# Head projections by pairs of output blocks, half of each sum by seven products of 256 tokens

## The chip, the cores and the metric

The kernel runs on one core of a Trainium2 chip. The metric is the device time of one execution in microseconds (us). A core has five engines that run side by side: PE multiplies matrices (128 x 128 weights against up to 512 columns, sums in PSUM), DVE and ACT work element by element on SBUF and PSUM, POOL does so on SBUF and issues transfers, SP issues transfers.

## The reference, cut to what matters

A decoder block on 512 tokens of width 2048, all in float32:

```python
hn = rmsnorm(h, norm1_g[l])
proj = hn @ w_in[l]                       # 2048 x 5656
(q_a, k_a, v_a, q_b, k_c, v_c, k_s, v_s, k_w, v_w, g_b) = jnp.split(proj, offsets, axis=-1)
o_a = dilated_mixture(...)                # 8 heads of 128
o_b = gates[..., 0:1] * o_cmp + gates[..., 1:2] * o_sel + gates[..., 2:3] * o_win   # 8 heads, 2 K/V groups
mixed = jnp.concatenate([rmsnorm(o_a, grp_norm_a[l]), rmsnorm(o_b, grp_norm_b[l])], axis=-1)
h = h + mixed @ w_out[l]
hn2 = rmsnorm(h, norm2_g[l])
h = h + (jax.nn.silu(hn2 @ w_gate[l]) * (hn2 @ w_up[l])) @ w_down[l]
return rmsnorm(h, final_g)
```

The compressed keys and values of mixer B come from `k_c` and `v_c` through a small two-layer network (weights `cmp_w1`, `cmp_w2`).

## The kernel before

**Precision.** Every operand of a large matrix product is kept as a high part and a rest (`wh`, `wl` for weights, `ah`, `al` for tokens), and a product is three matmuls: wh with ah, wh with al, wl with ah (`mm3`, `mm`). ACT makes the high part of a weight block (L143), DVE the rest (L146).

**The stream of weights.** All weights arrive in the order that `plan()` writes: units of 512 KB in one of five `raw` buffers, issued by SP (`load_to`). A unit is two halves; each half is a `Job` whose `first` (ACT) is written three halves ahead of its use and whose `second` (DVE) two halves ahead (`split_to`, called by `next_half`). `later(n, f)` puts other work n halves on. Every engine works through its own instructions strictly in the order written.

**The stages.** (1) The tokens are split into `ah`, `al` (16 slices of 128 features, 512 tokens each) while the projections for compression run. (2) The keys and values of the first group of mixer B (`ks`, `kw`, `vs`, `vw`), with sixteen units of compression weights (`w1_unit`) between their blocks. (3) The heads: for j from 0 to 7 four output blocks `qb`, `qa`, `ka`, `va`; at j = 4 also the second group's `ks`, `kw`, `vs`, `vw`. (4) The output projection, half of mixer B first (`out_unit(1)`) and that of mixer A afterwards. (5) The FFN, whose products are already formed by seven products of 256 tokens instead of eight (Strassen's scheme in Winograd's form: weight blocks and token blocks are added first, the quarter results afterwards). (6) The final norm.

**Stage 3 closely.** A block is one PSUM bank (`proj_block`, two of them) that takes 16 slices x 3 matmuls of 512 columns (`in_unit`, `run_unit`). After every six matmuls `side_hook` runs one `step()` of the attention: scores (`Att.s`), softmax rows on DVE and ACT, transposes (`Att.t`), the product with the values (`pv`). `evac` and `evac_v` take a finished block out of PSUM. When a head is done, `head_done` copies its output to `osb`, an SBUF tile that holds all sixteen, and sums its squares on POOL (L707). In the last block the outputs of mixer B are scaled and split into `ah`, `al` (`split_act`, L290 and L291), where the output projection reads them; after the last attention step (`close_attention`) those of mixer A follow.

Of the kernel before, what the change touches and what calls it, by code (L numbers as in the profile page):

```python
# [11 lines left out]
F32 = mybir.dt.float32  # L12
F32R = mybir.dt.float32r
AF = mybir.ActivationFunctionType
# [27 lines left out]

def plan():
# [9 lines left out]
    for j in range(NH):  # L53
        if j == 4:
            for name in ("ks", "kw", "vs", "vw"):
                for half in range(2):
                    p.append(("in", name, 1, half))
        for name in ("qb", "qa", "ka", "va"):
            for half in range(2):
                p.append(("in", name, j, half))  # L60
# [12 lines left out]

@with_exitstack
def block_kernel(ctx: ExitStack, tc: tile.TileContext, xt, wst, wdn, smalls, wg, w2c, bias, ident_in, out):
# [8 lines left out]
    mem = ctx.enter_context(tc.tile_pool(name="mem", bufs=1, space=bass.MemoryType.DRAM))  # L84
    kept_hs = [mem.tile([128, S], F32, name=f"res{nb}") for nb in range(KB)]
# [44 lines left out]
    class Job:  # L130
# [3 lines left out]
        def __init__(self, src, prep=None, post=None, load=None, dst=None, even=False):  # L134
            self.src, self.prep, self.post, self.load, self.dst, self.even = src, prep, post, load, dst, even

        def first(self):
            if self.load:
                self.load()
            if self.prep:  # L140
                self.prep()
            self.h, self.l = self.dst() if self.dst else wsplit(self.even)
            act.activation(self.h, self.src(), AF.Copy)  # L143

        def second(self):
            dve.tensor_tensor(self.l, self.src(), self.h.bitcast(F32), op=OP.subtract)  # L146
            if self.post:
                self.post()
# [27 lines left out]

    for u, d in enumerate(units):
        if d[0] not in ("quad", "dn"):
# [3 lines left out]
    n_plain = len(jobs)  # L182
    k = 2 * units.index(("out", 0, 1))
# [16 lines left out]

    pos = {"half": 0}
    side_hook = [lambda: None]

    def next_half():
# [3 lines left out]
        if i < n_plain:  # L208
            load_to(i // 2 + LA)
# [78 lines left out]
    def split_act(i, src, gain):  # L288
# [7 lines left out]
    osb = ap_.tile([128, KB, S], F32, name="osb")  # L296
# [9 lines left out]
    w2 = osb[:, 0, :].rearrange("p (a b) -> p a b", a=4)  # L306
    hids = osb[:, 1, :].rearrange("p (s h) -> p s h", s=2)
    hidt = [osb[:, 2, :128].rearrange("p (a r b) -> p a r b", a=2, r=1),
            osb[:, 3, :384].rearrange("p (a g r b) -> p a g r b", a=2, g=2, r=3)]
# [80 lines left out]

    def task():
        (tasks.popleft() if tasks else kv_low)()
# [79 lines left out]

    def evac(p, tag, scale=None, keep=False):
# [13 lines left out]
    def evac_v(p):  # L487
        t = tmp()
        dve.tensor_tensor(t, p, r1, op=OP.mult)
        return t  # L490
# [18 lines left out]
    class Att:  # L509


        def __init__(self, kind, q, k, v, bias_t, gate, o, first, last, done=None):
            self.kind, self.q, self.k, self.v, self.bias = kind, q, k, v, bias_t
            self.gate, self.o, self.first, self.last, self.done = gate, o, first, last, done
            self.e = {}
            self.s_steps = [self.cmp_s] if kind == "cmp" else [lambda: self.s([3]), lambda: self.s([2]),
                                                               lambda: self.s([1, 0])]
            self.t_steps = [self.cmp_t, self.cmp_pv] if kind == "cmp" else [
                lambda: self.t([3]), lambda: self.t([2]), lambda: self.t([1, 0]), self.pv]

# [9 lines left out]
        def s(self, tiles):  # L530
# [30 lines left out]
            later(0, rows)  # L561

        def t(self, tiles):
            p = ps.tile([128, 512], F32, tag="t", name="pt", bufs=2)
# [30 lines left out]
        def cmp_s(self):  # L595
# [23 lines left out]
            later(0, rows)  # L619

        def cmp_t(self):
            p = ps.tile([128, 512], F32, tag="t", name="pt", bufs=2)
# [6 lines left out]
        def cmp_pv(self):  # L629

            self.o["p"] = ps.tile([128, 512], F32, tag="o", name="po")
            pe.matmul(self.o["p"], self.v(), et_h[:96, 0:4, :], start=True, stop=False)

# [63 lines left out]
    def head_done(i, grp):  # L697
        def f(p):
            act.activation(osb[:, i, :], p, AF.Copy)
# [12 lines left out]

    kv = {}
    n1 = 0

    def kv_group(g, w1):
        nonlocal n1
        for name in ("ks", "kw", "vs", "vw"):
            p = proj_block()
            for half in range(2):  # L720
                in_unit(p, half)
# [11 lines left out]
            if name[0] == "k":  # L733
                kv[name] = evac(p, name)
            else:
                kv[name] = V()
                t = evac_v(p)
                queue.append(lambda t=t, name=name, v=kv[name]: setattr(v, "x", v_turn(t, name)))
# [13 lines left out]
    for j in range(NH):  # L752
# [5 lines left out]
        p = proj_block()  # L758
        for half in range(2):
            in_unit(p, half)  # L760
        q = evac(p, "qb", SCALE, True)
        o = {}
        queue.append(Att("cmp", q, kc[:, 32 * g:32 * g + 32],
                         V(et_h[:96, 7 + 3 * g, :]), bb, 3 * j, o, True, False))
        queue.append(Att("sel", q, kv["ks"], kv["vs"], bb, 3 * j + 1, o, False, False))
        queue.append(Att("win", q, kv["kw"], kv["vw"], bb, 3 * j + 2, o, False, True, head_done(8 + j, 1)))
        p = proj_block()
        for half in range(2):
            in_unit(p, half)
        q = evac(p, "qa", SCALE)  # L770
        p = proj_block()
        for half in range(2):
            in_unit(p, half)
        k = evac(p, "ka")
        v = V()
        queue.append(Att("dil", q, k, v, ba, None, {}, True, True, head_done(j, 0)))
        p = proj_block()
        for half in range(2):
            in_unit(p, half)
            if j == NH - 1 and half == 0:  # L780
                cur["late"] = 1
                for i in range(8):
# [760 lines left out]
```

## Time and profile before

| | |
|---|---|
| median of 3 runs | 2131.9 us (2131.46 to 2132.48) |
| profiled execution | 2134.17 us, its span 2132.1 us |
| granted PE clock | 0.998 |
| busy: PE, DVE, ACT, POOL | 2119.3, 1654.0, 1259.9, 316.9 us |
| moved from and to memory | 245.43 MB read, 65.01 MB written |

The span reaches from the first to the last instruction. A busy share is an average over stages; what an engine costs is read within one stage. The start times of two matmuls that follow each other without a wait give PE's real pace; their durations overlap. In the heads the tile names are `pp` (projection blocks), `psc` (scores), `pt` (transposed probabilities), `po` (head outputs), `pv` (transposed values); `pab` is the output projection, `phid` the compression, `P` and `pd` the FFN.

### The profile page before, as it was taken

To read this page: it belongs to the slowest core of one execution; us is meant where nothing else is said; L and a number is where in the kernel's file an instruction comes from. 1 tells how busy PE (TensorE), PEld (TensorE's weight loads), DVE (VectorE), ACT (ScalarE), POOL (GpSimd) and SP (SyncE) were. 2 spreads that over 40 slices of the span, in tenths; PEclk is the share of its full clock that TensorE was granted. 3 is DMA by queue.
4 is the path that set the end of the run, shared out by engine and by line. 5 is a ranking of instruction groups with operands and counts; after the bars stand their busy time and mean duration, and the time that the engine had idled before them with its cause. 6 is when DMAs were issued, how large, how long until landed. Compare 5 with 4: busy or idle time off the path is not lost.

```text
span 2132.1 us, 41370 instructions
## 1 busy us (share of the span) xinstructions
PE 2119.3 (99%) x15298; PEld 1980.7 (93%) x15298; DVE 1654.0 (78%) x3540; ACT 1259.9 (59%) x3059; POOL 316.9 (15%) x375
## 2 busy tenths in 40 slices
PE   9999999999999999999999999999999999999997
PEld 8888888888888888999999999999999999999997
DVE  6755656366557678998989888988888898988885
ACT  6544444244445246576676758585757667675856
POOL 0000000000000002011131413130312212030323
PEclk9999999999999999999999999999999999999999
DMA  7442222321224336356695959694756757494982
GB/s 238 145 144 82 82 82 70 101 82 51 87 95 148 99 99 171 119 164 197 150 208 152 231 138 221 154 206 131 186 145 169 180 139 185 138 218 118 210 245 92
DMA packets 122907, 313.13 MB, mean 147 GB/s; under 512 B 13264, under 2 KB 35408, under 8 KB 122704
## 3 DMA queue, kind: packets, MB, share of 16 engines
q1 hardware_dynamic: 75952, 236.49, 34.8%
q0 software_dynamic: 46608, 73.95, 19.5%
q8 instruction: 119, 1.95, 0.4%
q14 instruction: 84, 0.69, 0.1%
q10 hardware_dynamic: 144, 0.07, 0.0%
HBM read 245.43 MB, written 65.01 MB: 146 GB/s over the span
## 4 chain that ended last, share of the span: by engine, by line
PE 99%; DVE 0%; issue 0%; ACT 0%; DVEq 0%
PE P L1224 18%; PE P L1223 18%; PE P L1222 18%; PE pp L197 7%; PE pp L199 7%; PE pp L198 7%; PE pab L198 3%; PE pab L199 3%; PE pab L197 3%; PE pd L1222 1%; PE pd L1224 1%; PE pd L1223 1%; PE pt L568 1%; PE pl L198 1%; PE po L198 1%; PE po L197 1%
## 5 line engine op out<-in xcount | busy, mean ns | idle before, releaser
L143 ACT ACTIVATE wh<-raw 128x512 fp32r<-128x512 f32 x888 | 533.0, 625 | 279.1 <-DVE raw L810 118.9
L146 DVE TENSOR_TENSOR wl<-raw,wh 128x512 fp32r<-128x512 f32 x888 | 598.7, 685 | 101.5 <-ACT wh L143 98.5
L1224 PE MATMUL P<-ah,wl 128*128 128x256 f32 x1616 | 448.1, 277 | 0.0
L1222 PE MATMUL P<-ah,wh 128*128 128x256 f32 x1616 | 447.6, 277 | 0.0
L1223 PE MATMUL P<-al,wh 128*128 128x256 f32 x1616 | 447.3, 277 | 0.0
L1224 PEld LDWEIGHTS P<-ah,wl 128*128 128x128 f32 x1616 | 303.5, 188 | 0.7 <-DVE wl L146 0.2
L1222 PEld LDWEIGHTS P<-ah,wh 128*128 128x128 f32 x1616 | 303.5, 188 | 0.0
L1223 PEld LDWEIGHTS P<-al,wh 128*128 128x128 f32 x1616 | 303.5, 188 | 0.0
L1144 POOL DMA_DIRECT2D sums<-stg x240 | 201.0, 889 | 429.1 <-ACT P L1137 150.9
L197 PE MATMUL pp<-ah,wh 128*128 128x512 f32 x640 | 260.5, 407 | 0.0
L199 PE MATMUL pp<-ah,wl 128*128 128x512 f32 x640 | 250.9, 392 | 0.0
L198 PE MATMUL pp<-al,wh 128*128 128x512 f32 x640 | 250.2, 391 | 0.0
L170 DVE TENSOR_TENSOR wl<-raw,wh 128x256 fp32r<-128x256 f32 x480 | 186.5, 419 | 30.0 <-ACT wh L166 28.1
L810 DVE TENSOR_TENSOR raw<-raw 128x512 f32<-128x512 f32 x274 | 188.1, 686 | 3.6
L166 ACT ACTIVATE wh<-raw 128x256 fp32r<-128x256 f32 x480 | 176.6, 409 | 4.8 <-DVE raw L886 4.8
L199 PEld LDWEIGHTS pp<-ah,wl 128*128 128x128 f32 x640 | 120.2, 188 | 28.3 <-DVE wl L146 0.4
L197 PEld LDWEIGHTS pp<-ah,wh 128*128 128x128 f32 x640 | 120.5, 188 | 20.0 <-DVE tmp L369 0.5
L198 PEld LDWEIGHTS pp<-al,wh 128*128 128x128 f32 x640 | 120.6, 188 | 19.5
L555 ACT ACTIVATE e<-e,st 128x512 f32<-128x512 f32 (+1 forms) x96 | 53.7, 560 | 124.2 <-DVE st L549 124.2
L1137 ACT ACTIVATE stg<-P 128x256 f32<-128x256 f32 x280 | 106.7, 382 | 14.2 <-PE P L1224 2.7
L707 POOL TENSOR_TENSOR acc<-acc,osq 128x512 f32<-128x512 f32 x14 | 18.1, 1290 | 580.3 <-ACT osq L706 580.3
L197 PE MATMUL pab<-ah,wh 128*128 128x512 f32 x256 | 100.3, 392 | 0.0
(343 smaller groups left out, 5394.2 us busy)
## 6 DMA issues: line engine op xcount, KB each, us to landing
raw<-in_wst_dram SPq DMA_DIRECT2D x390, 512.0 KB, 4.2
sums<-stg POOLq DMA_DIRECT2D x160, 256.0 KB, 6.6
raw<-in_wst_dram POOLq DMA_DIRECT2D x40, 256.0 KB, 4.6
sums<-stg POOLq DMA_DIRECT2D x80, 128.0 KB, 6.2
bias<-in_bias_dram SPq DMA_DIRECT2D x16, 320.0 KB, 2.9
xc<-in_xt_dram SPq DMA_DIRECT2D x16, 256.0 KB, 3.0
hs<-in_xt_dram SPq DMA_DIRECT2D x16, 256.0 KB, 5.8
res<-hs POOLq DMA_DIRECT2D x16, 256.0 KB, 6.4
```

The costliest lines, as they stand in the source:

```text
L143: act.activation(self.h, self.src(), AF.Copy)
L146: dve.tensor_tensor(self.l, self.src(), self.h.bitcast(F32), op=OP.subtract)
L166: act.activation(h, src(), AF.Copy)
L170: dve.tensor_tensor(l, src(), h.bitcast(F32), op=OP.subtract)
L197: pe.matmul(o, wh, mh, start=start, stop=False)
L198: pe.matmul(o, wh, ml, start=False, stop=False)
L199: pe.matmul(o, wl, mh, start=False, stop=stop)
L810: return lambda: dve.tensor_tensor(o(), o(), x(), op=OP.add)
L1144: return lambda s=sums[x]: pool_e.dma_start(kept_sums[k][:, q:q + n, :], s, **how)
L1222: pe.matmul(o, wh, mh, start=start, stop=False, skip_group_check=True)
L1223: pe.matmul(o, wh, ml, start=False, stop=False, skip_group_check=True)
L1224: pe.matmul(o, wl, mh, start=False, stop=stop, skip_group_check=True)
```

## The change

In stage 3 two output blocks go together: (`qb`, `qa`), (`ka`, `va`), and for the second group (`ks`, `kw`), (`vs`, `vw`). Of the length of their sums the lower half (feature slices 0 to 7) is formed by seven products with 256 tokens, each over four slices; the upper half stays four jobs with 512 tokens (X0, X1, Y0, Y1), added to the same PSUM banks. The order in a pair is P1, P6, P7, P5, X0, P2, X1, P3, P4, Y0, Y1. Block x is complete after P3, block y after Y1 (with its sign turned, which `evac` undoes).

What belongs to that: the weight blocks are added on DVE (`pair_jobs`); quarter results are copied by ACT and added by DVE (`pair_unit`). The combined token blocks are formed once, in stage 2: the first eight slices are loaded again, by POOL's queue, scaled, combined and split in four rounds of three steps (`mix_parts`), one step at each call of the hook between the blocks `kw`, `vs` and `vw`; T1's splits follow in the last block. They occupy six tiles (T2h to T4l) in SBUF. The room comes from `osb`: each head's output now lies in one tile `oh` and is written to memory (`kept_o`); after P4 of the last pair it is read back into those six tiles (`place`), by POOL's queue. The softmax rows are written one job later inside the short products, or at the transposes that need them (`scaled`).

The core of the diff:

```diff
+def pair_units(x, y, i):
+    return [("pair", x, y, i, 0), ("pair", x, y, i, 1), ("in", x, i, 1), ("in", y, i, 1)]
...
+    PAIR = ("P1", "P6", "P7", "P5", "X0", "P2", "X1", "P3", "P4", "Y0", "Y1")
+    def pair_jobs(u):
+        a11, a21, a22, a12 = half_of(u, 0), half_of(u, 1), half_of(u + 1, 0), half_of(u + 1, 1)
+        def sums():
+            load_to(u + 2)
+            for n in ("s1", "s2"):
+                pair[n] = ap_.tile([128, 512], F32, tag=n, name=n)
+            dve.tensor_tensor(pair["s1"], a21(), a22(), op=OP.add)
+            dve.tensor_tensor(pair["s2"], pair["s1"], a11(), op=OP.add)
+        def grow(o, a):
+            return lambda: dve.tensor_tensor(o(), o(), a(), op=OP.add)
+        def more(n):
+            return lambda: load_to(u + n + 1)
+        js = {"P1": Job(a11, prep=sums, post=grow(a11, a21)), "P6": Job(s2), "P7": Job(a11, post=more(RB)),
+              "P5": Job(lambda: pair["s1"]), "P2": Job(a12, post=grow(a12, s2)), "P3": Job(a12),
+              "P4": Job(a22, post=more(RB + 2))}
...
+    def mix_load(i):
+        for n, k in (("s1", i), ("s2", 4 + i)):
+            pair[n] = ap_.tile([128, 512], F32, tag=n, name=n)
+            pool_e.dma_start(pair[n], xt[k])
+    def mix_parts(i):
+        x, y = pair["s1"], pair["s2"]
+        def m1():
+            act.activation(x, x, AF.Copy, scale=sm[:, SM_G1 + i:SM_G1 + i + 1])
+            act.activation(y, y, AF.Copy, scale=sm[:, SM_G1 + 4 + i:SM_G1 + 5 + i])
+            dve.tensor_tensor(quarter_sums[:, i, :], x[:, LO], x[:, HI], op=OP.subtract)
+            dve.tensor_tensor(y[:, HI], y[:, HI], x[:, HI], op=OP.subtract)
+        def m2():
+            high("T3", y[:, HI])
+            dve.scalar_tensor_tensor(x[:, HI], y[:, HI], -1.0, x[:, LO], op0=OP.mult, op1=OP.subtract)
+            dve.scalar_tensor_tensor(x[:, LO], x[:, HI], -1.0, y[:, LO], op0=OP.mult, op1=OP.subtract)
+            high("T2", x[:, HI])
+        def m3():
+            low("T3", y[:, HI])
+            high("T4", x[:, LO])
+            low("T2", x[:, HI])
+            low("T4", x[:, LO])
+            if i < 3:
+                mix_load(i + 1)
+        return [m1, m2, m3, lambda: None]
...
+    def pair_unit(x, y, at=None, dense=False):
+        a, b = proj_block(), proj_block()
+        for name in PAIR:
+            h, l = next_half()
+            now_in[0] = 1 if name[0] == "P" else 0
+            if name[0] == "P":
+                p, c = lo_hi[name]
+                th, tl = mixed[operand[name]]
+                for k in range(4):
+                    mm(p[:, c], h[:, 128 * k:128 * k + 128], l[:, 128 * k:128 * k + 128], th[:, k, :], tl[:, k, :],
+                       name in ("P1", "P7") and k == 0, False)
+                    if k == 3 or k == 1 and (dense or name in ("P1", "P4")):
+                        side_hook[0]()
...
+            if name == "P6":
+                s = ap_.tile([128, 4, 256], F32, tag="slots", name="slots")
+                act.activation(s[:, :2, :], a.rearrange("p (i c) -> p i c", c=256), AF.Copy)
+            elif name == "P5":
+                act.activation(s[:, 2:, :], b.rearrange("p (i c) -> p i c", c=256), AF.Copy)
+            elif name == "P2":
+                dve.tensor_tensor(s[:, 1:4:2, :], s[:, 1:4:2, :], s[:, :1, :].to_broadcast([128, 2, 256]), op=OP.add)
+                dve.tensor_tensor(s[:, 2, :], s[:, 2, :], s[:, 1, :], op=OP.add)
+            elif name == "P3":
+                dve.tensor_tensor(a[:, HI], a[:, HI], s[:, 3, :], op=OP.add)
+                x(a)
+            elif name == "P4" and at:
+                at()
+        bv = b.rearrange("p (i c) -> p i c", c=256)
+        dve.tensor_tensor(bv, bv, s[:, 1:3, :], op=OP.add)
+        y(b)
...
+    def place(tag, *blocks):
+        t = ap_.tile([128, 1088], F32, tag=tag, name="back")
+        for n, i in enumerate(blocks):
+            places[i] = t[:, 512 * n:512 * n + 512]
+            if i != 7:
+                osb[i] = places[i]
+                pool_e.dma_start(osb[i], kept_o[i])
...
     def head_done(i, grp):
         def f(p):
-            act.activation(osb[:, i, :], p, AF.Copy)
+            osb[i] = o = back(7) if i == 7 else ap_.tile([128, S], F32, tag="oh", name="oh")
+            act.activation(o, p, AF.Copy)
+            if i not in (7, 15):
+                pool_e.dma_start(kept_o[i], o)
...
+    def last_pair():
+        place("T2h", 8, 9)
+        place("T2l", 10, 11)
+        place("T3h", 12, 13)
+        place("T3l", 14, 7)
+        place("T4h", 0, 1)
+        place("T4l", 2, 3)
+        cur["late"] = 1
+        for i in range(8):
+            later(3 if i == 7 else i // 2, lambda i=i: split_act(i, osb[8 + i], sm[:, SM_GB + i:SM_GB + i + 1]))
+        later(3, lambda: place("T2h", 4, 5))
+        later(3, lambda: place("T2l", 6))
...
+                if name == "kw" and half:
+                    mix_load(0)
+                    mixes.extend(m for i in range(4) for m in [lambda i=i, n=n: mix_step(i, n) for n in range(4)])
+                if name == "vw" and half:
+                    while mixes:
+                        task()
+                    for i in range(4):
+                        later(i // 2, lambda i=i: mix_first(i, 0))
+                        later(1 + i // 2, lambda i=i: mix_first(i, 1))
...
+        end = j == NH - 1
+        pair_unit(take_qb, lambda p: took.update(q=evac(p, "qa", -SCALE)), dense=end)
+        pair_unit(take_ka, take_va, last_pair if end else None, end)
```

201 lines of the change are left out of this document (136 added, 65 removed).

## The prediction

> **What bounds the kernel now.** I read the page's busy times and the chain that ended last first, then the busy time by stretch, then the spacing of the matmuls.
>
> ```profile
> PE 2119.3 (99%) x15298; PEld 1980.7 (93%) x15298; DVE 1654.0 (78%) x3540; ACT 1259.9 (59%) x3059; POOL 316.9 (15%) x375
> PE 99%; DVE 0%; issue 0%; ACT 0%; DVEq 0%
> 150.00:350.00 200.00, 200.00 (x1017) 168.24 (x1016) 121.44 (x345) 89.66 (x231) 5.13 (x4) 1.00 0.24 79
> 76.70:120.00 43.30, 43.12 (x252) 37.77 (x251) 29.75 (x49) 26.10 (x48) 0.00 (x0) 1.00 0.71 231
> 640.00:690.00 50.00, 50.00 (x259) 42.36 (x259) 36.25 (x85) 27.72 (x54) 2.64 (x2) 1.00 0.46 158
> 880.00:2100.00 1220.00, 1219.97 (x10640) 1218.63 (x10640) 1069.39 (x2172) 836.81 (x2112) 276.04 (x320) 1.00 0.70 172
> ```
>
> The four stretches (length, then busy PE, weight loads, DVE, ACT, POOL, clock, DMA share, GB/s) are the heads, the compression stage before them, the passage from heads to output projection, and the FFN. PE is the bound in all of them, at clock 1.00. So time goes away only with PE work, and any new wait of PE is paid in full. DVE is busy for 61% of the heads (121.44 of 200) and for 88% of the FFN (1069.39 of 1220), where PE still loses nothing: a full DVE queue alone does not stall PE.
>
> **The PE work taken out.** Of each matmul row the start time is what counts.
>
> ```profile
> 500.03 0.40 PE L197 MATMUL pp<-ah,wh 128*128 128x512 f32 x1
> ...
> 503.95 0.39 PE L199 MATMUL pp<-ah,wl 128*128 128x512 f32 x1
> 517.42 0.40 PE L197 MATMUL pp<-ah,wh 128*128 128x512 f32 x1
> ...
> 519.92 0.40 PE L199 MATMUL pp<-ah,wl 128*128 128x512 f32 x1
> 1300.26 0.28 PE L1222 MATMUL P<-ah,wh 128*128 128x256 f32 x1
> ...
> 1306.15 0.28 PE L1223 MATMUL P<-al,wh 128*128 128x256 f32 x1
> ```
>
> The first pair of rows lies 17 matmuls apart (3.92/17 = 230.6 ns), the second 11 (2.50/11 = 227.3 ns), the third 52 (5.89/52 = 113.3 ns). A product of 256 tokens thus costs half of one of 512, and no more. For one pair of blocks the lower half of the sum was 2 blocks x 8 slices x 3 = 48 matmuls of 512; it becomes 7 products x 4 slices x 3 = 84 of 256. That is 48 x 0.229 - 84 x 0.1133 = 10.99 - 9.52 = 1.47 us per pair. There are 18 pairs (2 for each of 8 heads, and 2 for the second group's keys and values): 26.5 us; by the two spacings of 512 it is 25.1 to 27.9.
>
> The Trainium skill (TensorE: Matmul & The Clock Gate, "Wait — 56ns, not 53.3ns?") speaks against halving: a warm matmul costs N/2.4 ns and a fixed 2.5 ns besides. By it the term would be 48 x 215.8 - 84 x 109.2 ns = 1.19 us a pair, 21.4 us in all. The spacings above show no such fixed part (two of 113.3 are 226.6), so I stay with 26.5.
>
> **What DVE and ACT get in the heads.**
>
> ```profile
> 164.58 16.31 SPq L506 DMA_DIRECT2D bias<-in_bias_dram  x2
> 225.63 16.31 SPq L506 DMA_DIRECT2D bias<-in_bias_dram  x2
> L143 ACT ACTIVATE wh<-raw 128x512 fp32r<-128x512 f32 x888 | 533.0, 625 | 279.1 <-DVE raw L810 118.9
> L146 DVE TENSOR_TENSOR wl<-raw,wh 128x512 fp32r<-128x512 f32 x888 | 598.7, 685 | 101.5 <-ACT wh L143 98.5
> L810 DVE TENSOR_TENSOR raw<-raw 128x512 f32<-128x512 f32 x274 | 188.1, 686 | 3.6
> L883 DVE TENSOR_TENSOR s<-raw 128x256 f32<-128x256 f32 x80 | 33.7, 422 | 1.4
> L699 ACT ACTIVATE osb<-po 128x512 f32<-128x512 f32 x14 | 8.4, 599 | 29.9 <-PE po L199 29.9
> ```
>
> Two biases are loaded once a head, so a head lasts 61.05 us; DVE is busy 0.607 x 61.05 = 37.1 us of it, ACT 0.448 x 61.05 = 27.4. Per pair DVE gets three more weight splits (11 jobs for 8: 3 x 0.685), four sums of weight blocks (4 x 0.686), and the sums of quarter results: two of 512 (2 x 0.69) and two of 256 (2 x 0.42). Together 2.06 + 2.74 + 2.22 = 7.0 us. ACT gets 3 x 0.625 and two copies from PSUM (2 x 0.60): 3.1 us. Per head, then, DVE 37.1 + 14.0 = 51.1, ACT 27.4 + 6.2 = 33.6, PE 61.05 - 2 x 1.47 = 58.1. DVE stands at 88%, the share at which the FFN runs without a stall.
>
> The order within a pair matters as well. A weight split is written two jobs ahead of its use. The tightest place is P3, P4, Y0: after P3's last matmul DVE must add a quarter (0.42), scale and split block x (2 x 0.69 and ACT's 0.6 between), form the next pair's sums (1.37) and split Y1 (0.69), about 4.5 us, beside about 1.2 for the attention step. PE has P4 and Y0 until then, 1.36 + 2.75, and three or four attention steps of about 0.5 each ((61.05 - 192 x 0.229)/32): 6 us. That just covers. Where an attention step is a heavy one it won't. I take 2 us over the 18 pairs, with ends 0 and 10.
>
> The remaining edits in the heads cost nothing: SP's loads are the same four units a pair and are asked for at least five jobs ahead; each head's 256 KB written to memory is one issue on POOL, which is busy for 5.13 of 200 us; the one buffer `oh` is used again only when the next head's output ends, tens of us later. Both PSUM blocks of a pair are held to its end, but the second is first needed by P7, two products and their steps (about 4 us) after Y1, and its sum and scaling take 1.4.
>
> **The preparation, between 77 and 120 us.**
>
> ```profile
> 82.16 0.28 PE L427 MATMUL phid<-wh,kvs 128*128 128x256 f32 x1
> ...
> 85.01 0.39 PE L197 MATMUL pp<-ah,wh 128*128 128x512 f32 x1
> PEld phid L428 <- DVE wl L146: 0.4, 1, 0.4
> PEld pp L199 <- DVE wl L146: 0.4, 1, 0.4
> raw<-in_wst_dram POOLq DMA_DIRECT2D x40, 256.0 KB, 4.6
> L1321 POOL DMA_DIRECT2D res<-hs x16: 540/694/892, 838.2 to 848.8; - x16
> ```
>
> The mixed token blocks T1 to T4 are formed in four rounds here. A round is 7 DVE operations of 256 (2.9 us) and on ACT two scaled copies of 512 and three of 256 (about 2.5 us); T1's splits come at the end. In all DVE gets 4 x 2.9 + 4 x 0.42 = 13.4 us in a stretch where it is busy 29.75 of 43.3: full to the brim. And it is uneven: between blocks lie bursts of compression weights, six halves in 2.85 us (the first two rows), 0.475 each, while DVE needs 0.685 for each split, and in this stretch PE already waits for splits (0.4 us twice). Each of the rounds 2 to 4 also waits for its tokens: their buffers come free at the end of the round before, then two issues on POOL (2 x 0.69) and 4.6 us to landing, some 7.5 us with the tail of the round, against 5.5 us of PE between. ACT stands still for about 2 us, and behind it the splits for the next burst. I take 1.5 us three times, 5 us in all with what DVE's load adds; ends 0 (the splits ahead cover) and 12 (each burst pays 3 to 4). The first pair's sums fall into the last burst: 1 us more (0 to 2.5).
>
> The Trainium skill (DMA: Bandwidth & Descriptors, "Issuing engines are not separate DMA queues") says that loads issued from POOL interleave with SP's on the same 16 engines. By it the tokens would come later than 4.6 us here, where the DMA share is 0.71; the trace of before has no POOL load in this stretch.
>
> **The passage at the end of the heads.**
>
> ```profile
> L706 ACT ACTIVATE osq<-po 128x512 f32<-128x512 f32 x12 | 7.1, 593 | 0.0
> 671.66 1.29 POOL L707 TENSOR_TENSOR acc<-acc,osq 128x512 f32<-128x512 f32 x1 [10.93 <-ACT osq L706]
> L290 ACT ACTIVATE ah<-osb,sm 128x512 fp32r<-128x512 f32 x4 | 2.6, 708 | 0.0
> L291 DVE SCALAR_TENSOR_TENSOR al<-osb,sm,ah 128x512 fp32r<-128x512 f32 x4 | 2.8, 747 | 1.8 <-ACT ah L290 1.8
> xc<-in_xt_dram SPq DMA_DIRECT2D x16, 256.0 KB, 3.0
> res<-hs POOLq DMA_DIRECT2D x16, 256.0 KB, 6.4
> ```
>
> Before, the outputs of the B heads lay in SBUF when the output projection began. Now they are read back, and POOL's queue gets to that only behind the sum of squares of head 15, which the program puts ahead of it. From the end of that head's last product: copy and square 2 x 0.6, sum 1.29, issue 0.69, landing 4.6: 7.8 us, and 1.45 for its split: 9.2. PE has until then Y0 and Y1 (24 x 0.229) and two score steps (about 1.2): 6.7 us. So PE waits about 2.5 us for the first head. The DVE instructions behind the waiting split come late too: four subtractions (3.0), softmax steps (1.3), a weight split, the block's sum and its scaling (3 x 0.69), before the second output block has a PSUM bank: some 2 us more. I take 4; with the 3.0 of SP's reads instead of 4.6 it is 2, with the 6.4 of writes 7. The heads of mixer A are read back behind these, with 20 us of output products as cover.
>
> **The sum.** 26.5 - 2 - 5 - 1 - 4 = 14.5 us off. The profiled execution took 2134.17 us (span 2132.1 and 2.1 around it) and so comes to 2119.7; the median of the runs shown, 2131.9, comes to 2117.4. That is the forecast.
>
> **Rivals.** *All covered:* the lookahead hides the preparation and the passage, 0 to 6 us lost: 2105 to 2112. For it speaks that PE in 880 to 2100 never waits beside a fuller DVE; against it that POOL's order at the passage is fixed. *DVE paces the heads (slower):* DVE is in order, and of its 24 us idle per head some is spent waiting for ACT.
>
> ```profile
> DVE et_l L577 <- ACT et_h L576: 62.9, 66, 3.9
> DVE e L549 <- PE psc L199: 49.0, 62, 1.5
> DVE qbl L484 <- ACT qbh L483: 18.2, 8, 2.9
> DVE et_h L627 <- ACT et_h L626: 10.3, 8, 1.8
> ```
>
> If the waits on ACT of these rows stayed (91.4 us over 8 heads, 11.4 each), a head would take 51.1 + 11.4 = 62.5 us, 1.5 longer than now; over 8 heads and the pairs of the second group some 13, and with 10 for both ends 2155. From 9.9 us of such waits per head the heads gain nothing. Against it: most of these waits are ACT waiting for PE's transposes, and go when DVE comes late. *The ends eat the gain:* preparation and passage cost 22 to 30 us, because PE waits for each round's load whole: 2128 to 2136, no difference. *A fixed part per matmul:* if each of the 36 x 18 = 648 added matmuls cost 8 ns beyond its columns, 5.2 us would go and the time be 2122.6, inside the forecast's spread; against it, two of 113.3 make 226.6, under both spacings of 512. The rule of the Trainium skill given above (TensorE: Matmul & The Clock Gate, "Wait — 56ns, not 53.3ns?") would bring about this case.
>
> **Chances.** About 0.2% (4.3 us) is what can be told from no change. Forecast with its spread (2113 to 2124) 0.55; all covered 0.17; fixed part 0.03; ends dearer than I think but not all of the gain (2124 to 2127) 0.07: faster 0.82. Ends eat the gain 0.08. DVE paces 0.10. The range 2106 to 2129 takes the bounds of the ends and leaves out DVE pacing, most of "no difference" and the last of "all covered", 0.2 in all.
>
> **What would show it.** Right: PE starts in the 256 products 113 ns apart; a head of about 58 us between two bias loads; DVE near 88% there; PE's idle or stretched spacing only at 85 to 120 and at the first output blocks, where PE waits for the split of a head behind a load. Wrong: PE waiting for weight splits inside every pair, or a head of 61 us or more; a spacing above 113 ns in the products; waits of over 10 us in the preparation.

## The result, and the profile after

The kernel after takes 2178.15 us (median of 4 runs, 2176.49 to 2183.26); the kernel before, measured beside it, 2131.71 (2131.46 to 2132.48). The ratio is 1.0221, with a 95% interval of 1.0203 to 1.024: slower, by 46 us. The forecast was 2117.4, faster. The profiled execution has a span of 2174.8 us for 2132.1 before, 42.7 more. Spans are compared below, one profiled execution each, with the medians beside them; the four executions of after differ by up to 6.8 us, so a few microseconds between two spans mean little.

From the page of after, the busy times and the chain that ended last:

```profile
PE 2119.1 (97%) x15946; PEld 2000.2 (92%) x15946; DVE 1776.4 (82%) x3770; ACT 1315.3 (60%) x3173; POOL 332.9 (15%) x411
PE 82%; DVE 12%; ACT 3%; issue 2%; DMA 0%; POOL 0%; DVEq 0%; ACTq 0%; POOLq 0%
```

PE was 99% of the chain and is 82% now: what ends last runs for 15% of the span through DVE and ACT. By stretch (length, then busy PE, weight loads, DVE, ACT, POOL, clock, DMA share, GB/s), the preparation, the heads, the passage and the FFN:

```profile
60.00:150.00 90.00, 84.34 (x477) 72.37 (x476) 70.85 (x131) 56.71 (x109) 4.77 (x11) 0.98 0.53 177
150.00:640.00 490.00, 462.51 (x2921) 407.95 (x2921) 368.06 (x917) 238.46 (x582) 23.42 (x26) 1.00 0.26 86
640.00:720.00 80.00, 70.37 (x389) 58.89 (x388) 53.74 (x139) 40.96 (x93) 10.19 (x16) 0.96 0.41 134
920.00:2140.00 1220.00, 1219.97 (x10655) 1218.85 (x10655) 1072.20 (x2177) 836.92 (x2114) 272.31 (x320) 1.00 0.69 172
```

The FFN is as before. PE stands still in the other three, for 27.5 of 490 us in the heads, though DVE is at only 75% there (368.06 of 490). The two bias loads of a head, from SP's timeline, now lie 63.96 us apart, for 61.05 before and 58.1 forecast:

```profile
184.78 11.04 SPq L667 DMA_DIRECT2D bias<-in_bias_dram  x2
248.74 0.42 SPq L667 DMA_DIRECT2D bias<-in_bias_dram  x1
```

The chain of waits says for what, in 140 to 660 us, where PE's weight loads waited for nothing before (line of the waiting tile, whom for; total us, times, longest):

```profile
PEld po L242 <- ACT et_h L750: 13.7, 8, 1.8
PEld pt L800 <- issue: 11.1, 7, 1.7
PEld psc L776 <- DVE tmp L640: 6.2, 8, 0.8
PEld psc L243 <- DVE kal L645: 3.8, 7, 0.5
PEld psc L242 <- ACT kah L644: 2.1, 7, 0.4
PEld pp L249 <- DVE wl L155: 1.1, 3, 0.8
PEld pp L249 <- DVE wl L153: 0.5, 1, 0.5
```

The view has three more rows, and all ten come to 42 us. Waiting for weight splits (`wl`), which the prediction had looked at, is 1.6 us of them. Nearly all the rest are steps of the attention: values (`po`, 13.7 us) for ACT's copy of the transposed probabilities, transposes of the compressed probabilities (`pt` L800, 12.7 us with one of those three, in the matmuls' own rows behind DVE's `ecs`), scores (`psc`, 12.1 us) for the block just finished. One such step, from the timeline, behind the first pair of a head:

```profile
513.14 1.08 PE L776 MATMUL psc<-kc,tmp 128*128 128x32 f32 x8 [0.62 <-DVE tmp L640]
513.77 0.69 DVE L645 TENSOR_TENSOR qbl<-tmp,qbh 128x512 fp32r<-128x512 f32 x1 [0.69 <-ACT qbh L644]
514.38 0.68 DVE L198 TENSOR_TENSOR s<-raw 128x512 f32<-128x512 f32 x1
515.10 0.69 DVE L199 TENSOR_TENSOR s<-s,raw 128x512 f32<-128x512 f32 x1
515.71 0.68 DVE L153 SCALAR_TENSOR_TENSOR wl<-raw,wh 128x512 fp32r<-128x512 f32 x1
516.32 0.18 DVE L778 CUSTOM_DVE_ANT_0 ec<-psc,bias 128x31 f32<-128x31 f32 x1
...
518.50 1.08 DVE L789 TENSOR_SCALAR ecs<-ec,stc,gates 128x93 f32<-128x93 f32 x4
518.99 0.96 PE L800 MATMUL pt<-ident,ecs 128*96 128x128 f32 x4 [1.20 <-DVE ecs L789]
```

PE has the scores done at 514.2. DVE, in order, first forms the next pair's two sums (L198, L199) and a weight split (L153): 1.94 us, from 514.38 to 516.32, before it touches the scores. The transposes that need them stand 1.20 us idle.

### The profile page after: what moved, and what is told of

Same layout as the page of the kernel before. It is cut to its first block, busy times and chain, and to the rows that moved or that the text cites. A ratio compares the mean times of both kernels' runs of the same rounds, so it can differ in the third digit from the quotient of the medians.

```text
span 2174.8 us, 43202 instructions
## 1 busy us (share of the span) xinstructions
PE 2119.1 (97%) x15946; PEld 2000.2 (92%) x15946; DVE 1776.4 (82%) x3770; ACT 1315.3 (60%) x3173; POOL 332.9 (15%) x411
## 4 chain that ended last, share of the span: by engine, by line
PE 82%; DVE 12%; ACT 3%; issue 2%; DMA 0%; POOL 0%; DVEq 0%; ACTq 0%; POOLq 0%
PE P L249 18%; PE P L247 18%; PE P L248 18%; PE pab L242 3%; PE pab L244 3%; PE pab L243 3%; PE pp L249 3%; PE pp L247 2%; PE pp L248 2%; DVE wl L155 2%; PE pd L247 1%; PE pd L249 1%; DVE et_l L751 1%; PE pd L248 1%; DVE e L721 1%
## 5 line engine op out<-in xcount | busy, mean ns | idle before, releaser
L149 ACT ACTIVATE wh<-raw 128x512 fp32r<-128x512 f32 x906 | 545.5, 625 | 290.2 <-DVE raw L1028 122.7
L247 PE MATMUL pp<-ah,wh 128*128 128x512 f32 (+1 forms) x576 | 201.1, 349 | 0.0
L249 PE MATMUL pp<-ah,wl 128*128 128x512 f32 (+1 forms) x576 | 194.3, 337 | 0.1
L248 PE MATMUL pp<-al,wh 128*128 128x512 f32 (+1 forms) x576 | 193.2, 335 | 0.0
L249 PEld LDWEIGHTS pp<-ah,wl 128*128 128x128 f32 x576 | 108.1, 188 | 14.3 <-DVE wl L153 0.5
L248 PEld LDWEIGHTS pp<-al,wh 128*128 128x128 f32 x576 | 108.6, 188 | 9.1
L247 PEld LDWEIGHTS pp<-ah,wh 128*128 128x128 f32 x576 | 108.6, 189 | 9.0
L243 PE MATMUL pab<-al,wh 128*128 128x512 f32 x256 | 100.8, 394 | 0.6 <-DVE al L341 0.6
```

Of the source, the lines that this page charges most:

```text
L149: act.activation(self.h, self.src(), AF.Copy, scale=self.sign)
L243: pe.matmul(o, wh, ml, start=False, stop=False)
L247: pe.matmul(o, wh, mh, start=start, stop=False, skip_group_check=True)
L248: pe.matmul(o, wh, ml, start=False, stop=False, skip_group_check=True)
L249: pe.matmul(o, wl, mh, start=False, stop=stop, skip_group_check=True)
```

## The experiments

Two theories to begin with. *Closer steps*: the hook inside P1 and P4 puts two attention steps 0.70 us apart (six matmuls of 256), where before there were always 1.37 between, so the second finds its operands unfinished. *DVE's work*: 7 us more a pair, in order ahead of the softmax instructions, delays them. The ends (preparation, read-back) are a third part. "After" is the span of 2174.8 us. Each ratio is to the kernel before, measured again beside the run (medians 2132.3 to 2132.9 us).

**1. In P1 and P4, too, a step after the fourth slice only.**

```diff
-                    if k == 3 or k == 1 and (dense or name in ("P1", "P4")):
+                    if k == 3 or k == 1 and dense:
```

> In P1 and P4 only one attention step is run (after the last of the twelve matmuls), as in the other short products; 15 steps a pair instead of 17. Theory SPACING (PE waits in the heads because steps that stand 0.68 us apart in P1 and P4 come before DVE and ACT have finished the step before): the waits of po for et_h (13.7 us), of the compressed scores for the block (6.2) and of their transposes (12.7) go for the most part, 25 to 30 us off, about 2150 us. Theory LOAD (PE waits because DVE has 7 us more work per pair and both DVE and ACT work strictly in order, so each step's results come late wherever the step stands): only the 6 us of the compressed scores go, about 2171 us, and the other waits stay or move to other steps.

2159.87 us, ratio 1.0128 (1.0112 to 1.0143); span 2156.5, 18.3 less, between the two expectations. The waits of PE in 140 to 660 us fall from 42 to 27 us.

**2. No weight sums on DVE** (2.76 us a pair). The products take single weight blocks in their place.

```diff
-            dve.tensor_tensor(pair["s1"], a21(), a22(), op=OP.add)
-            dve.tensor_tensor(pair["s2"], pair["s1"], a11(), op=OP.add)
...
-        js = {"P1": Job(a11, prep=sums, post=grow(a11, a21)), "P6": Job(s2), "P7": Job(a11, post=more(RB)),
+        js = {"P1": Job(a11, prep=sums), "P6": Job(a21), "P7": Job(a11, post=more(RB)),
```

> Leaves out the four additions of weight blocks on DVE in every pair (P6 and P5 use single blocks instead of sums); splits, products and steps stay as they are, so the output is another. DVE gets 2.74 us less per pair, 49 us in all. LOAD: PE's waits at the attention steps shrink by half or more, 25 to 35 us off, about 2148 us. SPACING: 0 to 8 us off, about 2174 us.

2145.28 us, ratio 1.0059 (1.0043 to 1.0076); span 2142.5, 32.9 less. A head takes 59.9 us, and its waits for `po` fall to

```profile
PEld po L234 <- ACT et_h L742: 2.7, 2, 1.7
```

The steps stand as close as in after; with 2.8 us a pair off DVE most of their waits are gone (17 us in 140 to 660 us, for 42).

**3 and 4. The ends.** In 3 the forming of the mixed tokens is left out (their tiles are constant), in 4 the reading back (the splits read what lies in SBUF).

> Leaves out the forming of the mixed token blocks (loads, four rounds, T1's splits); the six tiles hold a constant set at the start by POOL, so the output is another. Both theories: the heads stay as they are. The last compression matmul came 7 us later than before and the first head's compressed scores 11.7 us later, of which 1.9 is their place in the order; so 7 to 10 us off, about 2169 us, and no clock drop at 90 to 100 us.

2170.47 us, ratio 1.0175 (1.016 to 1.019); span 2166.1, 8.7 less by the profile, 7.7 by the medians.

> Leaves out the read-back of the heads' outputs: the splits at the end of the heads read tiles that lie in SBUF already (the mixed tokens), so the output is another; the writes to memory stay. Both theories: the heads stay as they are; at the passage PE waited about 10 us (three waits for the split heads and what queues behind them) and ran some 7 us at the lower clock: 5 to 12 us off, about 2169 us. If the wait of 2.1 us for ka before the passage and the waits for the softmax rows stay, they belong to the heads' mechanism and not to the read-back.

2172.93 us, ratio 1.0192 (1.0177 to 1.0207), 5.2 less by the medians. That is less sure: the interval meets that of after (from 1.0203), and the span of its one profile (2174.6, at a granted clock of 0.995) shows nothing of it; its other three executions, at 0.997, have spans of 2170.6 to 2171.2. The heads' waits stay what they were in both. By the medians the ends cost 13 us.

**5. The two sums of P1 earlier**, behind X1's split in the pair before: written as X0 begins, four jobs ahead of their place in P4.

```diff
+        if units[u + 4][0] == "pair":
+            js["X1"].post = lambda: pair[u + 4]()
```

> The two sums s1, s2 of the next pair's weight blocks (1.37 us of DVE) are written after X1's split instead of in P4, behind block x; nothing is left out, DVE's total stays. If it is the crowded place P3, P4, Y0 that makes results late (the place which the prediction named as the tightest), the waits of the compressed scores' transposes (12.7 us) and of ka (6) shrink: 8 to 14 us off, about 2167 us. If DVE's total load counts and not the place: 0 to 3 us off, 2176 us. The wait of po for et_h in P1 stays in either case.

2170.78 us, ratio 1.018 (1.0163 to 1.0197); span 2167.9, 6.9 less, between the two expectations. The wait of the compressed transposes goes (12.7 to 2.1 us), and that of the values grows (13.7 to 16.2), presumably because the sums stand ahead of other steps now.

**6. Both ends earlier**: token loads two rounds ahead, the read-back of mixer B's heads after P7 of the last pair instead of P4.

> The preparation's tokens are loaded two rounds ahead into two sets of buffers, and the read-back of the B heads' outputs begins after P7 of the last pair instead of after P4; nothing is left out. By the runs without preparation (7.7 us) and without read-back (5.2 us) 13 us are the most that can go. If the preparation's price is the waiting for the loads, 5 of its 7.7 us go; if it is DVE's and ACT's own work there, 0 to 2. The passage: 4 to 5 us. Together 2166 to 2173 us.

2169.23 us, ratio 1.0172 (1.0157 to 1.0187); span 2168.1, 6.7 less, 8.9 by the medians: more than half of the ends' price, with nothing left out.

**7. A longer distance between dependent steps.**

```diff
-    SLACK = 2
+    SLACK = 3
```

> The attention's order waits for one more step between scores and transposes and between transposes and the product with the values (SLACK 3 for 2); the hooks stay where they are. LOAD and SPACING alike: a result has 0.7 to 1.4 us more time, so the waits of po (13.7) and of the compressed transposes (12.7) mostly go; the wait of the compressed scores for their block (6.2) stays. 15 to 25 us off, about 2158 us. If nothing is gained, the waits are no matter of time between steps, but each is moved on to the next step.

2163.42 us, ratio 1.0144 (1.0129 to 1.0159); 14.7 less by the medians. The waits of `po` fall from 13.7 to 1.2 us, those for the finished block (`tmp`) rise from 6.2 to 13.0.

**8 and 9. The same DVE work in the kernel before.** Run 8 adds one DVE instruction of 128x512 behind each split of the heads' blocks (5.5 us for two blocks), 9 as many, but four behind the first split of every block (144 in 36 places; "every second block" in the expectations is not what the edit does):

```diff
+                if d[0] == "in" and u > 31 and u % 2 == 0 and k == 0:
+                    jobs[-1].post = lambda j=jobs[-1]: [
+                        dve.tensor_tensor(j.src(), j.src(), j.src(), op=OP.add) for _ in range(4)]
```

> The kernel before, with one more DVE operation of 128x512 (0.686 us, a weight half that has been used up is added to itself) after each split of the heads' blocks: 5.5 us per pair of blocks, 98 us in all, DVE at about 79% in the heads. Steps, products and loads are as before. LOAD: PE begins to wait at attention steps, 8 to 25 us more, 2140 to 2157 us. SPACING: DVE has room, 0 to 3 us more, 2133 us.

2137.36 us, ratio 1.0024 (1.0014 to 1.0033), between the two expectations.

> The kernel before with as many added DVE instructions as in the run with one more add behind each split (144 adds of 128x512, about 98 us of DVE work; what they form is read by nothing), but four behind the first split of every second block, and none behind the others: 2.7 us of DVE work in one place, as the kernel after has three around P1. Spread evenly they cost 5 us. If the total of DVE's work is what counts, the same here: 2137 (+5, at most +10). If it is the work in one place, which stands in order ahead of a softmax step, each of the 36 places can delay the step behind it by up to 2.7 us less the slack that the evenly spread work showed: between 0.5 and 1.3 us each, +18 to +47 us, 2150 to 2179.

2134.11 us, ratio 1.0005 (0.9996 to 1.0015). So 98 us of DVE work cost the kernel before 5 us spread out and next to nothing bunched, less than either expectation of run 9 had. DVE's load alone is not the cause, nor is its crowding alone.

**10. Runs 1, 5 and 6 in one.**

> The kernel after with three edits together: steps in P1 and P4 after every fourth product again (measured alone: span 18.3 us less), the two sums of P1 formed during the pair before (7.4 less), both ends loaded earlier (8.9 less). If each of them takes away a loss of its own, the three add up: 34.6 us off the span of 2174.8, so 2140 us, a little above the kernel before. If the closer steps and the DVE work of the sums are one loss seen twice (a softmax step that comes late for the values of its block), the first two overlap and the sum falls short by up to 7 us: 2147. Faster than before (under 2127) on neither.

2158.27 us, ratio 1.0125 (1.011 to 1.014); span 2154.7: little more gained than by run 1 alone, and less than either expectation. The head takes 64 us again, with other waits:

```profile
PEld psc L779 <- DVE tmp L643: 13.1, 6, 2.5
PEld pp L252 <- DVE wl L155: 7.7, 13, 0.9
150.00:640.00 490.00, 471.50 (x2962) 422.81 (x2962) 369.82 (x924) 243.13 (x585) 23.52 (x26) 0.98 0.26 86
```

PE waits for less than in after (27 us for 42), but its clock is 0.98 in this stretch, for 1.00: 2% of 490 is 10 us.

**11. No weight sums, and steps after the fourth slice only** (runs 1 and 2 together).

> The four sums of weights of each pair are left out on DVE (the products use the weights as they are, so what the projections of the pairs compute is not the reference's) and the steps in P1 and P4 come after every fourth product. Alone the first took 32.9 us off the span and the second 18.3. If the two were independent losses: 2174.8 - 51.2 = 2124 us. If they are one loss seen from two sides, the head without sums (59.95 us) has only what is left of 1.9 us over the 58.1 that TensorE's products need: at most 15 us further, 2127, and if the closer steps cost nothing where DVE has time, no further than 2142. A head of 58.1 to 58.6 us would show that the time of the products was predicted rightly and everything lost in the heads is DVE work and places of steps.

2152.36 us, ratio 1.0096 (1.008 to 1.0113); span 2149.1, 6.6 longer than run 2. None of the expectations holds. Where the sums are gone, the closer steps cost nothing; without them PE waits for more (21.9 us for 17.1 in 140 to 660: `psc` for the finished block 8.2 for 6.2, `pp` for splits 4.6 for 0.9), and its clock in 150 to 640 us is 0.99 for 1.00. That the work moved there because two places a pair are missing is likely, not shown.

**12 and 13. Only one of the two closer steps.**

> The kernel after with the closer step kept in P4 and taken out of P1: 16 steps a pair, as many as the kernel before has for four blocks (after 17, the run with neither 15). If the place in P1, right behind the sums in DVE's order, is what costs, nearly all of the 18 us that both took comes back here: span 2155 to 2160, and the wait of the values for ACT's copy (14 us) and of the compressed transposes (11 us) goes. If only the number of steps counts, half: 2165. If it is P4: none, 2175.

2175.41 us, ratio 1.0195 (1.0181 to 1.0209); span 2173.5.

> The kernel after with the closer step kept in P1 and taken out of P4. The mirror of the run before: if P1 is the costly place, 2172 to 2178; if P4 is, 2155 to 2160; if the number counts, 2165.

2181.05 us, ratio 1.0226 (1.0213 to 1.024); span 2178.0. By its time neither place returns anything alone: each run fits one branch of its expectation, and the two branches contradict each other. The waits and the clock say more. In 140 to 660 us PE waits 32.1 us in run 12 and 40.5 in run 13, for 42.0 in after: without the closer step of P1 9.9 us of waits go, without that of P4 1.5. But in 150 to 640 us PE's clock is at one half for five stretches of 3.4 us in run 12 and three in run 13, and for none in after. The last section shows the first of them, where a matmul of 512 takes 0.43 us for 0.23; by that an estimate of the loss is 8 and 5 us. Together this gives 2 us less and 3 more, and the spans moved by 1.3 less and 3.2 more. In both runs the wait of the compressed transposes in the rows put to `issue` grows (from 11.1 to 18.6 and 16.1 us); perhaps with another count of steps they meet DVE's crowded places elsewhere.

**14 and 15. The sums by DMA** that adds into its target, P2 ahead of X0; 15 with the ends of run 6.

```diff
+                pool_e.dma_start(pair[n], wst[u][:, 512:1024])
+                pool_e.dma_start(pair[n], wst[u + 1][:, 0:512], accum_op=OP.add)
+            pool_e.dma_start(pair["s2"], wst[u][:, 0:512], accum_op=OP.add)
...
+            return lambda: pool_e.dma_start(o(), a(), accum_op=OP.add)
```

> All four weight sums of a pair are formed by DMA that adds into memory (seven transfers of 256 KB a pair on the queue that POOL issues), except those of the first pair's s1 and s2; DVE has none of the 2.8 us a pair. So that the last of them has time to land, P2 goes ahead of X0. If DVE's time for the sums is the loss, this comes out like the kernel without sums: span 2142 to 2150. If it is that a sum delays the split of its block, whoever forms it, the wait moves to the splits' weights (waits of TensorE for ACT's high part, behind a DMA of 2 us and more) and the span stays at 2165 or more. Added traffic is some 60 GB/s in the heads on 86; if it collides with the blocks' own loads, it is slower than after.

2197.12 us, ratio 1.0295 (1.028 to 1.0309); span 2195.3.

> The same with both ends loaded earlier as well (8.9 us alone). If the parts add up as load taken off DVE and load taken off the ends: 2142.5 - 8.9 = 2134 us of span, 2137 in all, within 0.4% of the kernel before. With TensorE's products as timed in these runs (0.1174 us for 256 tokens, 0.229 for 512) the gain that was to be had is 18 x (48 x 0.229 - 84 x 0.1174) = 20 us, of which the ends and the compressed step's wait leave few: under 2125 is expected on no theory.

2189.39 us, ratio 1.0257 (1.0243 to 1.0271). DVE is relieved (323.91 us of 490, for 368.06), but now ACT, in order too, waits for each sum to land. From the waits of run 14 in 150 to 640 us:

```profile
ACT wh L149 <- DMA raw<-raw: 40.8, 14, 4.6
ACT wh L149 <- DMA s<-in_wst_dram: 36.0, 14, 7.2
ACT wh L149 <- DMA raw<-s: 31.8, 14, 3.2
PEld po L253 <- ACT et_h L761: 21.5, 12, 3.0
```

109 us of ACT's time, with the copies of the transposes queued behind them: the wait for `po` is longer than in after. The second expectation of run 14 was right that a sum delays whoever splits it, and wrong on where: not the splits' users, the attention steps behind.

**16 and 17. Closer steps in the kernel before**, without and with the bunched DVE work of run 9.

```diff
-                if s % 2:
+                i = pos["half"] - 1
+                if s % 2 or s == 2 and i > 63 and i % 8 in (0, 6) and units[i // 2][0] == "in":
                     side_hook[0]()
```

> The kernel before with two more steps for every two blocks of the heads, each 0.69 us behind the one before it and ahead of the next, at the places of the pair's P1 and P4 (18 steps for two blocks instead of 16). If closer steps cost by themselves (the run with single steps in the pairs gave 18.3 us back), here too: 2145 to 2155. If they cost only where DVE comes late, nothing: 2128 to 2135.

2140.98 us, ratio 1.0038 (1.0023 to 1.0053): 8 us, between the two expectations. All that PE waits for in 140 to 660 us:

```profile
PEld pv L496 <- DVE tmp L490: 7.7, 7, 1.1
```

> The same with the added DVE work of the bunched run (four adds of 0.68 us behind the first split of every second block). If crowded DVE work and closer steps together are the cause of what the heads of the kernel after lose, some 30 to 46 us are lost here as well: 2160 to 2180. If their sum costs no more than each alone (0 and what the run beside it shows), under 2140: then the cause lies in the pair itself, in what only it has: two blocks' evacuations at its end, operands of its steps that come later, fewer microseconds between the projections' end and the first scores.

2163.75 us, ratio 1.0145 (1.0128 to 1.0162): 31 us. Alone the two cost 8 and 1; together 31. The head takes 65.00 us. The wait of run 16 stays, and one of after's three comes, the largest, that of the values for ACT's copy; those of the compressed transposes and for the finished block do not:

```profile
165.73 16.84 SPq L510 DMA_DIRECT2D bias<-in_bias_dram  x2
230.72 0.33 SPq L510 DMA_DIRECT2D bias<-in_bias_dram  x1
PEld po L200 <- ACT et_h L580: 19.5, 14, 2.0
PEld pv L499 <- DVE tmp L493: 7.7, 7, 1.1
PEld psc L200 <- DVE st L553: 4.8, 8, 0.6
```

How the two meet is seen in the timeline of run 17:

```profile
307.30 0.49 PE L572 MATMUL pt<-ident,e 128*128 128x128 f32 x3
307.31 2.87 DVE L183 TENSOR_TENSOR raw<-raw 128x512 f32<-128x512 f32 x4
...
310.62 0.42 DVE L581 TENSOR_TENSOR et_l<-pt,et_h 128x256 fp32r<-128x256 f32 x1
311.07 0.28 ACT L580 ACTIVATE et_h<-pt 128x128 fp32r<-128x128 f32 x1 [2.81 <-DVE et_l L581]
...
311.40 0.50 PE L200 MATMUL po<-et_h,vwh 128*128 128x512 f32 x1 [1.51 <-ACT et_h L580]
```

The transposes end at 307.8. Behind DVE's four adds its share of the splitting (`et_l`) is late, behind that ACT's last copy, and the product with the values, which a closer step has brought forward, waits 1.51 us. With the steps further apart (run 9) the same adds fit, and this is all that PE waits for in 140 to 660 us:

```profile
PEld po L200 <- ACT et_h L579: 1.6, 7, 0.2
```

**18. No sums of quarters on DVE** (2.24 us a pair). The blocks keep what the products leave in PSUM.

> The four DVE instructions a pair that add quarters of the output blocks are left out (2.24 us a pair; what the pairs' projections give is then not the reference's). If DVE's amount of work decides, this is to the weight sums (2.76 us a pair, 32.9 us back) as 2.24 to 2.76: 27 us back, 2148 of span. If the place decides, then what waits for the evacuations (compressed scores 6.2 us, window scores for the low part of k 3.8 us) goes and little else: 5 to 12 us back, 2163 to 2170.

2160.0 us, ratio 1.0131 (1.0116 to 1.0146); span 2158.2, 16.6 less, between the two expectations. The waits for the finished block fall from 12.1 to 2.5 us (6.2 to 2.5 for `tmp`, and those for `kah` and `kal` go), the others stay.

## Why the prediction was wrong, by its steps

**The failed step is the 2 us for the heads.** It asked whether DVE's weight splits keep ahead of PE, found one place where that "just covers", and took 2 us with an upper end of 10. The splits did keep ahead (1.6 us of waits). What it never costed was the other chain that DVE and ACT carry: scores, softmax, scaling, transposes, copy, values, whose every link on DVE and ACT stands in order behind whatever the pair put there. The places were there to be counted: the hooks in P1 and P4 stand in the quoted diff, and six matmuls of 256 are 0.7 us instead of 1.37 between steps that need each other.

How much: the span grew by 42.7 us; with 21 us of products saved (next point) and 13 for the ends, the heads lost about 51. PE's waits account for 42 of them; the rest is not attributed. Of the three waits, that of the values is shown by runs 9, 16 and 17: closer steps with bunched DVE work are enough for it, and for 31 us, in a kernel whose heads have no seven products. That of the compressed transposes goes with the place of the sums (run 5), that for the finished block with the sums of quarters (run 18). Taking work off DVE returns 32.9 (weight sums) and 16.6 (sums of quarters); they were not taken out together, and runs 10 and 11 show that such numbers need not add up.

**DVE's total was the wrong thing to fear and to trust.** "A full DVE queue alone does not stall PE" held (runs 8 and 9: 98 us more for 5 and 1 us), and so did the amount, roughly: 75% of a head of 64.0 us is 48 us of DVE for 51 forecast. What does not follow is that PE then loses nothing. The FFN, from which this was read, has no steps of the attention; in the heads each goes from PE through DVE and ACT back to PE, a few microseconds later.

**The gain was 21 us, not 26.5.** The products of 256 tokens in the heads run at two paces. The starts of PE's timeline, in the same pair, 11 and 9 matmuls apart:

```profile
497.05 0.28 PE L247 MATMUL pp<-T3h,wh 128*128 128x256 f32 x1
...
498.29 0.28 PE L249 MATMUL pp<-T3h,wl 128*128 128x256 f32 x1
...
499.09 0.28 PE L249 MATMUL pp<-ah,wl 128*128 128x256 f32 x1
...
500.15 0.28 PE L249 MATMUL pp<-ah,wl 128*128 128x256 f32 x1
```

1.24/11 is 112.7 ns and 1.06/9 is 117.8 ns. In 130 to 660 us the mean over 270 intervals that begin at an `al` matmul of 256 is 116.9 ns, over 214 that begin at a T2 one 117.0 (seven that took over 160 ns are left out); for 512 tokens it is 229.3 before (567 intervals). With 117.0, 48 x 0.2293 - 84 x 0.1170 is 1.18 us a pair, 21.2 us in all. Two products of 256 cost 4.7 ns more than one of 512. The prediction read 113.3 from one stretch of the FFN; 512 tokens showed 227 and 231 ns in its own rows, and it could have taken the same spread for 256. That is its rival of a fixed part per matmul, which had 5.2 us less for this (5.3 were missing) and 0.03 of chance. The rule of the Trainium skill (TensorE: Matmul & The Clock Gate, "Wait — 56ns, not 53.3ns?"), a fixed 2.5 ns per matmul, gave 21.4 us: nearer than the row that was preferred to it. That it comes so near is partly luck: its two terms, 215.8 and 109.2 ns, both lie 6 to 7% under the measured 229.3 and 117.0.

**The ends were about right.** Preparation 5 us forecast, 7.7 measured (the first pair's sums, 1 us, were not taken out by themselves); passage 4 forecast, 5.2 measured, within the doubt said above. The waits for splits between the bursts of compression weights came as described: `phid` waits for `wl` 5.3 us in 60 to 140 us, for 0.4 before. The rounds' tokens took 5.5 us to land, for 4.6 in the sum:

```profile
s<-in_xt_dram POOLq DMA_DIRECT2D x6, 256.0 KB, 5.5
```

A term that the sum lacked is the clock: it is at one half for 3.4 us from 95.3 and for 6.8 us from 696.0, together about 5 us by the paces of the last section.

**The slower rival was the nearest.** "DVE paces the heads" foresaw that instructions in order keep waiting for ACT and put a head at 62.5 us, the time at 2155. Measured were 64.0 and 2178. Its mechanism is half of what was found: DVE does not pace by its total, but by what stands ahead of a step. The reason against it, that the waits go when DVE comes late, left out that PE's transposes and values come later with them.

**Left open.** What exactly puts PE's clock at one half in the heads of some versions (runs 1, 7 and 10 to 15) and not in after's, which hides what the single closer steps are worth; where the last 9 us of the heads' loss lie; and what decides between 113 and 118 ns. No version tried reaches the kernel before; the nearest that computes everything is run 10, 1.25% slower.

## What to carry to other kernels

When products are shortened, count what rides on them: steps placed every so many products move closer together in time, and a distance kept in steps shrinks with them. Where an engine works in order, cost an added instruction by who stands behind it and how soon that is needed, not by the engine's share of busy time. Two changes that cost little by themselves (8 and 1 us here) can cost 31 together, so all edits that draw on the slack of one chain are to be costed together. And where a time does not move, read the waits and the granted clock apart: one can hide the other.

## What the runs showed of the hardware

A DVE instruction beside a POOL addition was stretched. From the timeline of after:

```profile
499.05 1.30 POOL L900 TENSOR_TENSOR acc<-acc,osq 128x512 f32<-128x512 f32 x1
499.21 1.70 DVE L155 TENSOR_TENSOR wl<-raw,wh 128x512 fp32r<-128x512 f32 x1 [1.73 <-ACT wh L149]
```

The split takes 1.70 us where it takes 0.68 elsewhere; POOL ends at 500.35, the split 0.56 later. All six weight splits that overlap such an addition in 150 to 640 us by more than 0.1 us took 1.70 to 1.99 us. The Trainium skill (SBUF — State Buffer, "Who interferes with whom") says that a DVE instruction with two inputs in SBUF contends with a GpSimd instruction that reads SBUF, and that one of the two is blocked while the other runs. The row agrees: most of the 0.68 came after POOL's end. Whether weight sums formed on POOL would only move DVE's loss was not tried.

PE's granted clock was at one half in some stretches of 3.4 or 6.8 us. In after it is so from 696.0, behind waits for the heads that are read back and for softmax rows, and the mean over 690 to 712 us is 0.84:

```profile
690.00:712.00 22.00, 18.73 (x77) 13.96 (x76) 15.63 (x35) 12.11 (x26) 4.76 (x9) 0.84 0.64 218
```

In the heads of run 12 the first follows a wait of PE's weight loads of 2.26 us, up to 216.7:

```profile
218.50:221.70 3.20, 3.20 (x9) 2.49 (x8) 1.99 (x4) 0.45 (x2) 0.00 (x0) 0.50 0.00 0
219.39 0.63 PE L242 MATMUL psc<-ksh,qbh 128*128 128x512 f32 x1
219.82 0.63 PE L243 MATMUL psc<-ksl,qbh 128*128 128x512 f32 x1
...
221.88 0.40 PE L247 MATMUL pp<-ah,wh 128*128 128x512 f32 x1
222.11 0.39 PE L248 MATMUL pp<-al,wh 128*128 128x512 f32 x1
```

The starts lie 0.43 us apart, and 0.23 right after. So a wait of PE can cost more than its length. Their sum does not decide: after's heads have 42 us of waits and a clock of 1.00, run 10's 27 us and 0.98. The length of a single wait may: the eight stretches in the heads of runs 12 and 13 lie at waits of 2.26 to 3.29 us, and after's heads, without any, have no wait over 1.8. But run 1 has one behind a wait of 1.49 us, so a bound is not shown.
